# Hybrid two-layer decoder trunk on one core: query phase loaded by alternating chunks in a fixed order, norm squares moved to ScalarE

## The chip, the core and the metric

The kernel runs on one core of a Trainium2 chip. The metric is device microseconds of one execution. The core has TensorE (PE, with its weight loads as PEld), VectorE (DVE), ScalarE (ACT), GpSimd (POOL) and SyncE (SP), which issues most transfers; ScalarE's queue issues the rest.

## The reference, cut to what matters

The input x is 512 x 1024 float32. Two layers follow each other, and each adds a mixer and a SwiGLU feed-forward network to x, both behind an RMS norm.

```python
def rms_norm(x, g):
    y = x * rsqrt(mean(x * x, axis=-1, keepdims=True) + EPS)
    return y * g
for layer in range(2):
    h = rms_norm(x, norm_mix[layer])
    x = x + (even_mixer(h, ...) if layer == 0 else odd_mixer(h, ...))
    h = rms_norm(x, norm_ffn[layer])
    x = x + (silu(h @ w_gate) * (h @ w_up)) @ w_down
```

The even mixer projects h to queries, keys and values of a stick-breaking attention and to the three inputs of a short gated convolution; the odd mixer selects the 128 best keys of each query and attends to them. So there are four norms: one of the input x, and three of a sum that the kernel has just made. We number these three A (layer 0 mixer to feed-forward 0), B (feed-forward 0 to layer 1 mixer) and C (layer 1 mixer to feed-forward 1).

## The kernel before, in words

**Number format.** Every float32 operand is split into a high and a low part, and a product is three matmuls (`mm3`, L102 to L106): high by high, high by low, low by high. Weights arrive as `raw`; `new_weights` (L143) issues the load on SP, ScalarE casts the high part `wh` (L149), VectorE or GpSimd subtracts the low part `wl` (L150). Three buffers each hold `raw`, `wh` and `wl`. Activations lie feature by token in `xT`, in eight chunks of 128 features; `split` (L166) makes a chunk's high part on ScalarE, scaled by the norm's gain (L174), and its low part on VectorE (L175). The factor 1/rms of a token is put in behind the matmuls, so that they need not wait for it.

**The start.** `setup` (L305) builds constants, loads the first gains and issues `WARM` matmuls of a constant. `layer0_mix` (L533) then runs the query phase. `load_x` (L372) loads x in four loads of 256 features, transposes each chunk on TensorE by four transposes (L382), splits it and copies it to `xT` on ScalarE (L385). The query projection takes weights in four loads of two chunks; for each it runs four output blocks m of 128 features, two chunks each, into four PSUM banks: 96 matmuls in all. Then `first_rstd` (L389) sums the squares of x on VectorE (L396, four instructions), takes the reciprocal root on ScalarE (L401) with a Newton step on VectorE (L281 to L283), and builds the row form `rbc` by four diagonal tiles (L409) and matmuls by ones (L411). `stack` (L414) takes each query block out of its bank by two ScalarE copies (L420) and two VectorE subtractions (L424). The next projection's first block (the keys, `k_proj`) uses the bank of query block 0. `setup_rest` (L336) loads the other gains by six transfers on ScalarE's queue and transposes them (L345).

**What sets the order.** A scheduler places each engine's instructions from the program's order and its own estimate of when each is ready. Only where a `manual_schedule` region is open (layer 1's mixer, L749) does each named engine keep the order in which the program issues; instructions from outside the region may still fall between them. `slot()` (L229) is called after each `mm3` of the later projections and runs what `after(n, ...)` has put n slots ahead.

**Norms A, B and C.** `residual_proj` (L646) adds each of the eight output chunks to `xT` (L655, L657), splits it for the next layer, and calls `stats_add` (L264): GpSimd squares the chunk (L268, L272) and adds it to `ssq` (L273); for the last chunk ScalarE squares (L275) and VectorE adds (L276). `rstd_mm` (L285) is put `LAGR_FFN` = 6 slots behind the projection for A and C, `LAGR_MIX` = 7 for B: a matmul by ones (L289) sums `ssq` over the partitions, and root and Newton step give `rbc`. Eight slots later `rstd_cols` (L296) turns it into columns `rcol` by four small matmuls (L300). Feed-forward 0 uses `rbc` alone.

Of the kernel before, what the change touches and what calls it, by code (L numbers as in the profile page):

```python
# [8 lines left out]
F32 = mybir.dt.float32  # L9
F32R = mybir.dt.float32r  # L10
ALU = mybir.AluOpType
# [4 lines left out]
P = 128  # L16
# [3 lines left out]
TB = S // P  # L20
HID = 2816
HC = HID // P
WARM = 24
ORDER = None
RATE0, LAG0 = 0.8, 5
LAGR_FFN, LAGR_MIX = 5, 7
L1_ORDER = {mybir.EngineType.PE, mybir.EngineType.DVE, mybir.EngineType.Activation,
            mybir.EngineType.Pool}
LAG_W, LAG_KI, LAG_DOT, LAG_CH, LAG_TK, LAG_TQ, LAG_T1, LAG_N, LAG_C, LAG_LO, LAG_P, EXPS = 3, 8, 5, 4, 8, 6, 4, 8, 11, 2, 3, 1
LAG_Z = 14  # L30
LAG_K, T1P, B2, LAG_KLO, P1 = 2, 3, 'adbc', 2, 0
EARLY, SQ_ACT = 3, 0
# [7 lines left out]
FILL = -3e38  # L40
TAKEN = -3.4e38
ARENA_KB = 104.5

EARLY = 2
T1P = 4
# [6 lines left out]
B2 = 'dbca'  # L52
LAG_N = 8
LAG_TK = 8
LAGR_FFN = 6
LAG_KLO = 1
LAG_Z = 14
LAG_W = 4
# [17 lines left out]
class Net:  # L76
# [64 lines left out]
                 2, 512, lo) for k0 in range(0, kc, 2)]  # L141

    def new_weights(self, src, kk, n, lo):  # L143
        nc = self.nc
        raw = self.wraw.tile([P, kk, n], F32, name="raw", tag="raw")
        nc.sync.dma_start(raw, src)
        wh = self.wsp.tile([P, kk, n], F32R, name="wh", tag="wh")
        wl = self.wsp.tile([P, kk, n], F32R, name="wl", tag="wl")
        nc.scalar.copy(wh, raw)  # L149
        (lo or nc.vector).tensor_tensor(wl, raw, wh.bitcast(F32), op=ALU.subtract)  # L150
        return wh, wl
# [109 lines left out]
            self.slot()  # L261


    def stats_add(self, c):  # L264

        nc = self.nc
        if c == 0:
            nc.gpsimd.tensor_tensor(self.ssq, self.xT[:, c], self.xT[:, c], op=ALU.mult)  # L268
            return
        sq = self.cst.tile([P, S], F32, name="sqx", tag="sqx")  # L270
        if c < KC - 1:
            nc.gpsimd.tensor_tensor(sq, self.xT[:, c], self.xT[:, c], op=ALU.mult)  # L272
            nc.gpsimd.tensor_tensor(self.ssq, self.ssq, sq, op=ALU.add)  # L273
        else:
            nc.scalar.activation(sq, self.xT[:, c], AF.Square)  # L275
            nc.vector.tensor_tensor(self.ssq, self.ssq, sq, op=ALU.add)  # L276

    def newton(self, y, v, t, src=None):

# [5 lines left out]
    def rstd_mm(self):  # L285
# [50 lines left out]
    def setup_rest(self):  # L336
        nc, I = self.nc, self.I
        rows = self.rows2
        nc.scalar.dma_start(rows[0:16, :], I["norm_ffn"].rearrange("l (c p) -> (l c) p", p=P))
        nc.scalar.dma_start(rows[16:28, :], I["ev_conv_w"][0].rearrange("w (c p) -> (w c) p", p=P))  # L340
        for j in range(2):
            nc.scalar.dma_start(rows[28:29, j * 64:(j + 1) * 64], I["od_q_gain"])
            nc.scalar.dma_start(rows[29:30, j * 64:(j + 1) * 64], I["od_k_gain"])
        ps = self.bank("z", "pstat")
        nc.tensor.transpose(ps[:, 0:30], rows[0:30, :], self.ident[0:30, 0:30])  # L345
        nc.vector.tensor_copy(self.cols[:, 16:46], ps[:, 0:30])
        nc.vector.tensor_scalar(self.cols[:, 46:47], self.cols[:, 44:45], 0.125, None, op0=ALU.mult)
# [21 lines left out]
            nc.scalar.dma_start(self.F, ft)  # L369


    def load_x(self, xp):  # L372

        nc = self.nc
        xr = self.I["x"].rearrange("o (b p) d -> p (o b) d", p=P)
        xt = xp.tile([P, TB, D], F32, name="x_tm")
        for i in range(4):
            nc.sync.dma_start(xt[:, :, i * 256:(i + 1) * 256], xr[:, :, i * 256:(i + 1) * 256])
            for c in (2 * i, 2 * i + 1):
                ps = self.bank("z", "pstat")  # L380
                for tb in range(TB):
                    nc.tensor.transpose(ps[:, tb * P:(tb + 1) * P], xt[:, tb, c * P:(c + 1) * P],  # L382
                                        self.ident)
                self.split(self.xh3(c), ps, g=self.g_mix(0, c))
                nc.scalar.copy(self.xT[:, c], ps)  # L385
            self.x_tm = xt
            yield

    def first_rstd(self, xp):  # L389
# [15 lines left out]
        dg = xp.tile([P, S], F32, name="dg")  # L405
        ps = self.bank("z", "pstat")
        for tb in range(TB):
            t = slice(tb * P, (tb + 1) * P)
            nc.vector.tensor_scalar(dg[:, t], self.ident, self.rcol[:, tb:tb + 1], None,  # L409
                                    op0=ALU.mult)  # L410
# [122 lines left out]
    def layer0_mix(self):  # L533
# [7 lines left out]
        heads = []  # L541
        with self.tc.tile_pool(name="xin", bufs=1) as xp:

            loads = self.load_x(xp)
            ps = [self.acc() for _ in range(4)]
            next(loads)
            for k0 in range(0, KC, 2):
                next(loads, None)
                wh, wl = self.weights(W[k0 * P:(k0 + 2) * P, 0:512].rearrange(
                    "(k p) n -> p k n", p=P), 2, 512)  # L550
                for m in range(4):
                    c = slice(m * P, (m + 1) * P)
                    for k in range(2):
                        h, l = xs[k0 + k]
                        self.mm3(ps[m], wh[:, k, c], wl[:, k, c], h, l, k0 + k == 0,
                                 k0 + k == KC - 1)
            self.first_rstd(xp)
            for m in range(4):
                qs = self.R(32 + 4 * m, 2, S)
                self.stack([(qs[0][:, e], qs[1][:, e]) for e in range(2)], ps[m])  # L560
                heads.append(qs[0])
        self.setup_rest()
        self.bias_table()

# [4 lines left out]
        with self.tc.tile_pool(name="l0", bufs=1) as sp:  # L569
# [67 lines left out]
            for j in range(4):  # L637
# [3 lines left out]
            self.few_banks(None)  # L641
            att = [(self.R(32 + 4 * i, S)[0], self.R(34 + 4 * i, S)[0]) for i in range(4)]
            self.residual_proj(I["ev_w_out"][0], att + conv, self.xh3,
                               lambda c: self.g_ffn(0, c), pair=2)

    def residual_proj(self, W, ins, out3, gain, scale_r=False, tmp=None, pair=1, part=False,  # L646
                      lo=None):

        nc = self.nc

        def ev(m, ps):
            if scale_r:
                t = tmp.tile([P, S], F32, name="rt", tag="ft")
                nc.vector.tensor_tensor(t, ps, self.rbc, op=ALU.mult)
                nc.vector.tensor_tensor(self.xT[:, m], self.xT[:, m], t, op=ALU.add)  # L655
            else:
                nc.vector.tensor_tensor(self.xT[:, m], self.xT[:, m], ps, op=ALU.add)  # L657
            if not part:
                self.split(out3(m), self.xT[:, m], g=gain(m))
                self.stats_add(m)  # L660
        self.proj_fm(W, 0, D, ins, ev, pair=pair, lo=lo)
        if not part:
            self.after(LAGR_MIX if scale_r else LAGR_FFN, self.rstd_mm)


    def ffn(self, layer, xs, g0):
# [5 lines left out]
        with self.tc.tile_pool(name=f"ffn{layer}", bufs=2) as fp:  # L672
# [30 lines left out]
            if not last:  # L703
                self.plan(self.fm_tiles(Wd, 0, D, HC, 256, 4, 1, None) + self.l1_tiles())
                self.residual_proj(Wd, gs, self.xh3, lambda c: self.g_mix(1, c), scale_r=True,
                                   tmp=fp)
                return
            for half in range(2):
                def ev_d(tb, ps):
# [21 lines left out]
    def layer1_mix(self):  # L731
# [15 lines left out]
        with ExitStack() as es:  # L747
# [331 lines left out]
            self.residual_proj(Wo[512:1024], half[4:8], lambda c: out3[c],  # L1079
                               lambda c: self.g_ffn(1, c))  # L1080
        self.ffn(1, [(o[0], o[2]) for o in out3], 0)


# [47 lines left out]
```

## Time and profile before

| what | us |
|---|---|
| median of 3 runs | 1231.54 (1231.36 to 1231.57) |
| the profiled execution | 1230.06 |
| its span, first to last instruction | 1228.3 |
| TensorE busy in it | 1196.7 (97%) |
| VectorE, ScalarE, GpSimd busy | 669.5, 466.2, 189.3 |

Times in the rows are microseconds from the span's start. A timeline row gives start, duration, engine, line, operation, output from inputs, shape, count, and in brackets the idle time before it and what ended that. Matmul durations overlap: the distance from one start to the next is the pace. A float32 operand without the split is run in two passes and shows as two records.

### The profile page before, as it was taken

To read this page: it belongs to the slowest core of one execution; us is meant where nothing else is said; L and a number is where in the kernel's file an instruction comes from. 1 tells how busy PE (TensorE), PEld (TensorE's weight loads), DVE (VectorE), ACT (ScalarE), POOL (GpSimd) and SP (SyncE) were. 2 spreads that over 40 slices of the span, in tenths; PEclk is the share of its full clock that TensorE was granted. 3 is DMA by queue.
4 is the path that set the end of the run, shared out by engine and by line. 5 is a ranking of instruction groups with operands and counts; after the bars stand their busy time and mean duration, and the time that the engine had idled before them with its cause. 6 is when DMAs were issued, how large, how long until landed. Compare 5 with 4: busy or idle time off the path is not lost.

```text
span 1228.3 us, 14473 instructions
## 1 busy us (share of the span) xinstructions
PE 1196.7 (97%) x5573; PEld 982.4 (80%) x5573; DVE 669.5 (55%) x1064; ACT 466.2 (38%) x755; POOL 189.3 (15%) x228
## 2 busy tenths in 40 slices
PE   9999999999999999999999889998999999999998
PEld 8787878788888888888787678887888888888886
DVE  6769965634343343444589988757444444342322
ACT  5656733332233222222263379654322222322120
POOL 1334303200000000122135444226000000000000
PEclk9999999999999999999999999999999999999999
DMA  6231223333333332232223221112333233323330
GB/s 206 68 91 53 60 79 97 92 94 95 103 86 103 92 97 94 95 95 87 86 89 93 77 70 35 53 50 88 86 88 101 87 103 86 103 90 99 111 112 35
DMA packets 103637, 108.32 MB, mean 88 GB/s; under 512 B 4660, under 2 KB 89696, under 8 KB 103568
## 3 DMA queue, kind: packets, MB, share of 16 engines
q1 hardware_dynamic: 102768, 106.21, 29.0%
q10 hardware_dynamic: 800, 1.18, 0.3%
q8 instruction: 44, 0.72, 0.2%
q14 instruction: 25, 0.20, 0.1%
HBM read 105.24 MB, written 2.14 MB: 87 GB/s over the span
## 4 chain that ended last, share of the span: by engine, by line
PE 79%; DVE 12%; issue 5%; ACT 2%; POOL 2%; DMA 1%; ACTq 0%; POOLq 0%; DVEq 0%
PE acc L104 20%; PE acc L106 20%; PE acc L105 20%; PE acc L220 4%; PE acc L219 4%; PE acc L221 4%; DVE wl L150 2%; DVE w L825 1%; DVE L L828 1%; PE pt L1009 1%; DVE arena L175 1%; DVE om L458 1%; DVE xT L657 1%; PE z L433 1%; PE po L105 1%
## 5 line engine op out<-in xcount | busy, mean ns | idle before, releaser
L104 PE MATMUL acc<-arena,wh 128*128 128x512 f32 (+2 forms) x1176 | 468.1, 398 | 1.4 <-DVE xT L657 1.0
L106 PE MATMUL acc<-arena,wl 128*128 128x512 f32 (+2 forms) x1176 | 459.8, 391 | 0.0
L105 PE MATMUL acc<-arena,wh 128*128 128x512 f32 (+2 forms) x1176 | 456.7, 388 | 1.4 <-DVE arena L175 1.3
L150 DVE TENSOR_TENSOR wl<-raw,wh 128x1024 fp32r<-128x1024 f32 (+1 forms) x175 | 220.8, 1262 | 347.3 <-ACT wh L149 347.2
L149 ACT CAST wh<-raw 128x1024 fp32r<-128x1024 f32 (+1 forms) x191 | 198.6, 1041 | 462.7 <-issue 196.5
L106 PEld LDWEIGHTS acc<-arena,wl 128*128 128x128 f32 (+1 forms) x1176 | 220.7, 188 | 50.3 <-issue 0.2
L105 PEld LDWEIGHTS acc<-arena,wh 128*128 128x128 f32 (+1 forms) x1176 | 221.1, 188 | 47.4 <-DVE arena L175 2.3
L104 PEld LDWEIGHTS acc<-arena,wh 128*128 128x128 f32 (+1 forms) x1176 | 221.1, 188 | 45.1 <-DVE xT L657 2.1
L219 PE MATMUL acc<-wh,arena 128*128 128x512 f32 x272 | 108.9, 400 | 0.3 <-DVE arena L175 0.3
L220 PE MATMUL acc<-wl,arena 128*128 128x512 f32 x272 | 108.2, 398 | 0.0
L221 PE MATMUL acc<-wh,arena 128*128 128x512 f32 x272 | 108.1, 397 | 0.0
L221 PEld LDWEIGHTS acc<-wh,arena 128*128 128x128 f32 x272 | 51.4, 189 | 12.2
L219 PEld LDWEIGHTS acc<-wh,arena 128*128 128x128 f32 x272 | 51.5, 189 | 12.1 <-DVE arena L175 0.7
L220 PEld LDWEIGHTS acc<-wl,arena 128*128 128x128 f32 x272 | 51.5, 189 | 11.5
L683 DVE TENSOR_TENSOR ft<-acc,rbc 128x512 f32<-128x512 f32 x44 | 30.5, 692 | 55.2 <-PE acc L106 55.0
L268 POOL TENSOR_TENSOR ssq<-xT 128x512 f32<-128x512 f32 x3 | 3.5, 1169 | 327.8 <-DVE xT L655 274.0
L150 POOL TENSOR_TENSOR wl<-raw,wh 128x1024 fp32r<-128x1024 f32 x16 | 38.9, 2430 | 69.3 <-ACT wh L149 67.8
L685 ACT ACTIVATE fs<-ft 128x512 f32<-128x512 f32 x44 | 27.5, 629 | 52.2 <-DVE ft L683 52.2
L690 DVE TENSOR_TENSOR fp<-acc,fs 128x512 f32<-128x512 f32 x44 | 30.4, 692 | 28.5 <-PE acc L106 28.5
L433 PE MATMUL z<-arena 128*128 128x384 f32 (+3 forms) x120 | 41.2, 346 | 4.8 <-DVE mx L976 2.8
L976 DVE CUSTOM_DVE_ANT_0 L<-z,bias 128x128 f32<-128x128 f32 (+3 forms) x64 | 30.7, 486 | 18.2 <-PE z L975 17.6
L986 ACT ACTIVATE L<-L,mx 128x128 f32<-128x128 f32 (+3 forms) x64 | 35.8, 560 | 11.9 <-DVE sm L993 9.4
(205 smaller groups left out, 1285.9 us busy)
## 6 DMA issues: line engine op xcount, KB each, us to landing
raw<-in_ffn_w_gate_dram SPq DMA_DIRECT2D x44, 512.0 KB, 3.8
raw<-in_ffn_w_up_dram SPq DMA_DIRECT2D x44, 512.0 KB, 3.7
raw<-in_ffn_w_down_dram SPq DMA_DIRECT2D x42, 512.0 KB, 3.7
raw<-in_ev_w_in_dram SPq DMA_DIRECT2D x24, 512.0 KB, 3.9
raw<-in_od_w_in_dram SPq DMA_DIRECT2D x16, 512.0 KB, 3.5
raw<-in_ev_w_out_dram SPq DMA_DIRECT2D x8, 512.0 KB, 3.4
bias<-F SPq DMA_DIRECT2D x16, 256.0 KB, 3.2
raw<-in_od_w_out_dram SPq DMA_DIRECT2D x8, 512.0 KB, 3.4
```

The lines of the kernel that those rows point to most:

```text
L104: mm(ps, wh, xh, start=first, stop=False)
L105: mm(ps, wh, xl, start=False, stop=False)
L106: mm(ps, wl, xh, start=False, stop=last)
L149: nc.scalar.copy(wh, raw)
L150: (lo or nc.vector).tensor_tensor(wl, raw, wh.bitcast(F32), op=ALU.subtract)
L219: mm(ps[tb], h[:, t], wh[:, k], start=c == 0, stop=False)
L220: mm(ps[tb], h[:, t], wl[:, k], start=False, stop=False)
L221: mm(ps[tb], l[:, t], wh[:, k], start=False, stop=c == kc - 1)
L433: self.nc.tensor.matmul(z, qs, kd, start=True, stop=False)
L683: nc.vector.tensor_tensor(t, ps, self.rbc, op=ALU.mult)
L976: nc.vector.tensor_tensor_reduce(out=u["ls"][:, r], in0=z, in1=bias[h][:, 0:nk][:, ::-1], scale=1.0, scalar=FILL, op0=ALU.add, op1=ALU.max ...
L986: nc.scalar.activation(ls[:, r], ls[:, r], AF.Exp, bias=mx[:, r:r + 1], accum_out=sm[:, r:r + 1])
```

## The change

x and the query weights come in turn by spans of 1, 1, 2, 2 and 2 chunks: all five x loads and the first three weight loads are issued at the start. The phase from the first transpose to `first_rbc` stands in a `manual_schedule` region for TensorE, VectorE, ScalarE and GpSimd: a span's transposes, splits and `xT` copies are issued after block m = 1 of the span before it, its weight casts only after them, and `first_rstd`'s sums of squares after all five spans. The row form's matmuls are issued after the `stack` calls. `setup_rest` first writes its tile from `rcol`, so its six transfers wait for `first_rstd`. `WARM` goes from 24 to 15. ScalarE makes all norm squares; GpSimd keeps the additions of chunks 0 to 6; in A and C the last chunk's square and addition are issued ahead of its split, and squares alternate between two buffers. `rstd_mm` is put 8 slots behind in A, 9 in B, 11 in C. A has no `rstd_cols`. The layer 1 key index waits 10 slots (`LAG_KI`) in place of 8.

```diff
-WARM = 24
+WARM = 15
-LAGR_FFN, LAGR_MIX = 5, 7
+LAGR_FFN, LAGR_MIX = 5, 9
...
+X_SPANS = ((0, 1), (1, 2), (2, 4), (4, 6), (6, 8))
...
-LAGR_FFN = 6
+LAGR_FFN = 8
...
-    def stats_add(self, c):
+    def stats_add(self, c, free):
         if c == 0:
-            nc.gpsimd.tensor_tensor(self.ssq, self.xT[:, c], self.xT[:, c], op=ALU.mult)
+            nc.scalar.activation(self.ssq, self.xT[:, c], AF.Square)
             return
...
+        sq = (self.rbc if free and c % 2 else
+              self.cst.tile([P, S], F32, name="sqx", tag="sqx"))
+        nc.scalar.activation(sq, self.xT[:, c], AF.Square)
+        (nc.gpsimd if c < KC - 1 else nc.vector).tensor_tensor(self.ssq, self.ssq, sq, op=ALU.add)
...
-        self.after(8, self.rstd_cols)
+        if cols:
+            self.after(8, self.rstd_cols)
...
     def setup_rest(self):
+        nc.vector.tensor_copy(rows, self.rcol[0:32, 0:1].to_broadcast([32, P]))
...
+    def load_x(self, xp, W):
+        for i, (a, b) in enumerate(X_SPANS):
+            c = slice(a * P, b * P)
+            nc.sync.dma_start(self.x_tm[:, :, c], xr[:, :, c])
+            if i < 3:
+                raws.append(self.load_raw(W[c, 0:512].rearrange("(k p) n -> p k n", p=P),
+                                          b - a, 512))
+        return raws
+    def turn_x(self):
+        for a, b in X_SPANS:
+            for c in range(a, b):
+                ps = self.bank("z", "pstat")
+                for tb in range(TB):
+                    nc.tensor.transpose(ps[:, tb * P:(tb + 1) * P],
+                                        self.x_tm[:, tb, c * P:(c + 1) * P], self.ident)
                 self.split(self.xh3(c), ps, g=self.g_mix(0, c))
                 nc.scalar.copy(self.xT[:, c], ps)
             yield
+    def queries(self, W, raws):
+        turns = self.turn_x()
+        self.qps = ps = [self.acc() for _ in range(4)]
+        next(turns)
+        for i, (a, b) in enumerate(X_SPANS):
+            raw = raws[i] if i < 3 else self.load_raw(...)
+            wh, wl = self.halves(raw, b - a, 512)
+            for m in range(4):
+                c = slice(m * P, (m + 1) * P)
+                for k in range(a, b):
+                    h, l = xs[k]
+                    self.mm3(ps[m], wh[:, k - a, c], wl[:, k - a, c], h, l, k == 0, k == KC - 1)
+                if m == 1:
+                    next(turns, None)
...
+            raws = self.load_x(xp, W)
+            with self.tc.manual_schedule(engines=L1_ORDER):
+                self.queries(W, raws)
+                dg = self.first_rstd(xp)
                 for m in range(4):
...
+                    self.stack([(qs[0][:, e], qs[1][:, e]) for e in range(2)], self.qps[m])
+                self.first_rbc(dg)
...
             if not part:
+                first = m == KC - 1 and not scale_r
+                if first:
+                    self.stats_add(m, not scale_r)
                 self.split(out3(m), self.xT[:, m], g=gain(m))
-                self.stats_add(m)
+                if not first:
+                    self.stats_add(m, not scale_r)
...
-            self.after(LAGR_MIX if scale_r else LAGR_FFN, self.rstd_mm)
+            self.after(lagr, lambda: self.rstd_mm(cols))
```

`halves` is the second part of `new_weights` (the two L149 and L150 instructions), `load_raw` the first. Layer 0's output projection passes `cols=False`, the down projection of feed-forward 0 passes `lagr=LAGR_MIX`, layer 1's last output projection passes `lagr=11`.

## Rows read from the trace of the kernel before

**Rows 1.** The page: busy time, and shares of the chain that ended last.
```profile
PE 1196.7 (97%) x5573; PEld 982.4 (80%) x5573; DVE 669.5 (55%) x1064; ACT 466.2 (38%) x755; POOL 189.3 (15%) x228
...
PE 79%; DVE 12%; issue 5%; ACT 2%; POOL 2%; DMA 1%; ACTq 0%; POOLq 0%; DVEq 0%
```

**Rows 2.** TensorE's timeline of the query phase and the matmul behind it.
```profile
13.35 0.66 PE L382 MATMUL pstat<-eye,x_tm 128*128 128x128 f32 x4 [0.41 <-ACT xT L385]
...
24.59 1.03 PE L382 MATMUL pstat<-eye,x_tm 128*128 128x128 f32 x8
...
25.69 0.40 PE L105 MATMUL acc<-arena,wh 128*128 128x512 f32 x1
...
36.23 0.39 PE L106 MATMUL acc<-arena,wl 128*128 128x512 f32 x1
36.46 1.05 PE L411 MATMUL pstat<-dg,ones 128*128 128x128 f32 x8
...
37.61 0.50 PE L104 MATMUL acc<-arena,wh 128*128 128x512 f32 x1
```

**Rows 3.** Busy time by window (us, instructions), granted clock, DMA share, GB/s: the start.
```profile
0.00:7.00 7.00, 5.88 (x31) 5.88 (x32) 0.68 (x3) 1.28 (x1) 3.56 (x11) 1.00 0.61 177
```

**Rows 4.** ScalarE's timeline: splits, copies and weight casts.
```profile
14.04 0.69 ACT L174 ACTIVATE arena<-pstat,cols 128x512 fp32r<-128x512 f32 x1 [0.26 <-PE pstat L382]
...
24.59 1.05 ACT L149 CAST wh<-raw 128x1024 fp32r<-128x1024 f32 x1 [2.13 <-PE acc L105]
25.55 1.26 ACT L174 ACTIVATE arena<-pstat,cols 128x512 fp32r<-128x512 f32 x2
...
28.23 1.06 ACT L385 COPY xT<-pstat 128x512 f32<-128x512 f32 x2
...
582.05 0.62 ACT L149 CAST wh<-raw 128x512 fp32r<-128x512 f32 x1 [4.40 <-PE acc L105]
```

**Rows 5.** VectorE's timeline in and behind the query phase.
```profile
21.75 1.22 DVE L396 CUSTOM_DVE_ANT_0 junk<-x_tm 128x1024 f32<-128x1024 f32 x1
...
23.01 1.23 DVE L396 CUSTOM_DVE_ANT_0 junk<-x_tm 128x1024 f32<-128x1024 f32 x1
...
25.67 1.23 DVE L150 TENSOR_TENSOR wl<-raw,wh 128x1024 fp32r<-128x1024 f32 x1 [1.23 <-ACT wh L149]
...
28.36 0.16 DVE L281 TENSOR_TENSOR t<-rcol 128x4 f32<-128x4 f32 x1
...
29.10 0.87 DVE L409 TENSOR_SCALAR dg<-eye,rcol 128x128 f32<-128x128 f32 x4
...
33.74 4.22 DVE L424 TENSOR_TENSOR arena<-acc,arena 64x512 fp32r<-64x512 f32 x6 [0.45 <-ACT arena L420]
```

**Rows 6.** Transfers issued before 60 us: tile, queue, KB, us to landing.
```profile
ssq<-in_norm_ffn_dram ACTq DMA_DIRECT2D x1, 8.0 KB, 4.0
```

**Rows 7.** TensorE's timeline at norm A.
```profile
235.14 1.12 PE L289 MATMUL pstat<-ssq,ones 128*128 128x512 f32 x2 [0.38 <-DVE ssq L276]
...
242.07 0.40 PE L106 MATMUL acc<-arena,wl 128*128 128x512 f32 x1
...
243.37 0.51 PE L104 MATMUL acc<-arena,wh 128*128 128x512 f32 x1
```

**Rows 8.** TensorE's timeline at norm B.
```profile
599.99 0.39 PE L104 MATMUL acc<-arena,wh 128*72 128x512 f32 x1
...
605.59 0.52 PE L104 MATMUL acc<-arena,wh 128*128 128x384 f32 x1
```

**Rows 9.** Busy time by window, columns as in rows 3: norms B and C.
```profile
603.00:607.00 4.00, 4.00 (x10) 2.67 (x11) 1.72 (x3) 1.62 (x3) 0.00 (x0) 0.57 0.00 1
...
853.00:859.00 6.00, 2.28 (x9) 1.25 (x8) 4.84 (x5) 3.36 (x4) 2.42 (x2) 1.00 0.22 57
```

**Rows 10.** TensorE's timeline at norm C.
```profile
853.79 0.39 PE L106 MATMUL acc<-arena,wl 128*128 128x512 f32 x1
857.90 1.13 PE L289 MATMUL pstat<-ssq,ones 128*128 128x512 f32 x2 [3.72 <-DVE ssq L276]
```

More of the change, by code (lines that the diff above doesn't have):

```diff
@@ L143, in new_weights, with load_raw, halves @@
     def new_weights(self, src, kk, n, lo):
+        return self.halves(self.load_raw(src, kk, n), kk, n, lo)
+    def load_raw(self, src, kk, n):
+        raw = self.wraw.tile([P, kk, n], F32, name="raw", tag="raw")
+        self.nc.sync.dma_start(raw, src)
+        return raw
+    def halves(self, raw, kk, n, lo=None):
         nc = self.nc
-        raw = self.wraw.tile([P, kk, n], F32, name="raw", tag="raw")
-        nc.sync.dma_start(raw, src)
         wh = self.wsp.tile([P, kk, n], F32R, name="wh", tag="wh")
@@ L283, in newton, with rstd_mm @@
         nc.vector.scalar_tensor_tensor(y, t, 1.5, y, op0=ALU.add, op1=ALU.mult)
-    def rstd_mm(self):
+    def rstd_mm(self, cols=True):
         nc = self.nc
@@ L369, in bias_table @@
             nc.scalar.dma_start(self.F, ft)
-    def load_x(self, xp):
+    def load_x(self, xp, W):
         nc = self.nc
         xr = self.I["x"].rearrange("o (b p) d -> p (o b) d", p=P)
[L376 to L379, printed above, removed]
+        self.x_tm = xp.tile([P, TB, D], F32, name="x_tm")
+        raws = []
+        for i, (a, b) in enumerate(X_SPANS):
[6 more added lines that the diff above has]
+    def turn_x(self):
+        nc = self.nc
+        for a, b in X_SPANS:
+            for c in range(a, b):
                 ps = self.bank("z", "pstat")
                 for tb in range(TB):
-                    nc.tensor.transpose(ps[:, tb * P:(tb + 1) * P], xt[:, tb, c * P:(c + 1) * P],
-                                        self.ident)
+                    nc.tensor.transpose(ps[:, tb * P:(tb + 1) * P],
+                                        self.x_tm[:, tb, c * P:(c + 1) * P], self.ident)
                 self.split(self.xh3(c), ps, g=self.g_mix(0, c))
                 nc.scalar.copy(self.xT[:, c], ps)
-            self.x_tm = xt
             yield
+    def queries(self, W, raws):
+        xs = self.xs
+        turns = self.turn_x()
+        self.qps = ps = [self.acc() for _ in range(4)]
+        next(turns)
+        for i, (a, b) in enumerate(X_SPANS):
+            raw = raws[i] if i < 3 else self.load_raw(W[a * P:b * P, 0:512].rearrange(
+                "(k p) n -> p k n", p=P), b - a, 512)
+            wh, wl = self.halves(raw, b - a, 512)
[3 more added lines that the diff above has]
+                    h, l = xs[k]
+                    self.mm3(ps[m], wh[:, k - a, c], wl[:, k - a, c], h, l, k == 0,
+                             k == KC - 1)
+                if m == 1:
+                    next(turns, None)
     def first_rstd(self, xp):
@@ L405, in first_rstd, with first_rbc @@
         dg = xp.tile([P, S], F32, name="dg")
+        for tb in range(TB):
+            nc.vector.tensor_scalar(dg[:, tb * P:(tb + 1) * P], self.ident,
+                                    self.rcol[:, tb:tb + 1], None, op0=ALU.mult)
+        return dg
+    def first_rbc(self, dg):
+        nc = self.nc
         ps = self.bank("z", "pstat")
@@ L542, in layer0_mix @@
         with self.tc.tile_pool(name="xin", bufs=1) as xp:
[L544 to L550, printed above, removed]
-                for m in range(4):
[L552 to L561, printed above, removed]
+            raws = self.load_x(xp, W)
+            with self.tc.manual_schedule(engines=L1_ORDER):
+                self.queries(W, raws)
+                dg = self.first_rstd(xp)
+                for m in range(4):
+                    qs = self.R(32 + 4 * m, 2, S)
+                    self.stack([(qs[0][:, e], qs[1][:, e]) for e in range(2)], self.qps[m])
+                    heads.append(qs[0])
+                self.first_rbc(dg)
         self.setup_rest()
@@ L643, in layer0_mix @@
             self.residual_proj(I["ev_w_out"][0], att + conv, self.xh3,
-                               lambda c: self.g_ffn(0, c), pair=2)
+                               lambda c: self.g_ffn(0, c), pair=2, cols=False)
     def residual_proj(self, W, ins, out3, gain, scale_r=False, tmp=None, pair=1, part=False,
-                      lo=None):
+                      lo=None, lagr=LAGR_FFN, cols=True):
         nc = self.nc
@@ L705, in ffn @@
                 self.residual_proj(Wd, gs, self.xh3, lambda c: self.g_mix(1, c), scale_r=True,
-                                   tmp=fp)
+                                   tmp=fp, lagr=LAGR_MIX)
                 return
@@ L1079, in layer1_mix @@
             self.residual_proj(Wo[512:1024], half[4:8], lambda c: out3[c],
-                               lambda c: self.g_ffn(1, c))
+                               lambda c: self.g_ffn(1, c), lagr=11)
         self.ffn(1, [(o[0], o[2]) for o in out3], 0)
```

11 lines of the change are left out of this document (1 added, 10 removed).

## The prediction

> **What bounds the kernel now.** I read the page first: TensorE is busy for 1196.7 of 1228.3 us, and the chain that ended last runs on it for 79% [rows 1]. So time changes only where the change makes TensorE wait or spares it a wait or an instruction. Then I read TensorE's timeline where the change touches it: the start and norms A, B, C. The query phase, once running, leaves no gap: from 25.69 to 36.23 lie 46 steps of 0.229 us, and 37.61 sees the key projection begin right behind the row form [rows 2]. At the norms it waits: 0.38 us in A [rows 7], 3.72 in C [rows 10], and in B it needs 5.4 us for five matmuls and a sum [rows 8], partly because the clock fell [rows 9]. ScalarE's and VectorE's timelines give the prices [rows 4, 5].
>
> **The start, step by step.** The order in the region is fixed, so I follow each engine through it.
> - Warm-up: 31 TensorE records begin before 7.00 [rows 3], which is 15 warm matmuls at two records each and one more. The gains' transpose follows, so span 1's transposes start at about 7.2.
> - A span's chain: from its first transpose to the split's begin 0.69 (13.35 to 14.04) [rows 2, 4]. Then ScalarE makes, per chunk, a high part (1.26 / 2 = 0.63) and a copy (1.06 / 2 = 0.53), and only then casts the weights: 0.62 for one chunk, 1.05 for two [rows 4]. That is 2.5 us for a span of one chunk, 4.1 for two. VectorE's low part of the weights takes 1.23 more for two chunks [rows 5], about half for one (estimate), and the third matmul needs it.
> - Span 1: first matmul at 7.2 + 2.5 = 9.7, then 0.2 for the low part.
> - What covers a later span's chain is its own transposes, 0.44 per chunk (25.69 - 0.229 is when the first matmul behind the eight transposes began, 0.88 after 24.59 [rows 2]), and blocks m = 2 and 3 of the span before: 6 matmuls (1.37) or 12 (2.75).
> - Span 2: 2.5 - 0.44 - 1.37 = 0.7, and 0.2 for the low part: 0.9. Span 3: 4.1 - 0.88 - 1.37 = 1.8, and 1.23 less two matmuls (0.46) = 0.8: 2.6. Spans 4 and 5: 4.1 - 0.88 - 2.75 = 0.4, and 0.8: 1.2 each.
> - End of the queries: 9.7 + 96 x 0.229 (22.0) + 28 transposes at 0.11 (3.1) + 0.2 + 0.9 + 2.6 + 2.4 = 40.9. Before, it is 36.46.
> - The tail: the last weights' low part ends 22 matmuls before that, at 35.9. Only then may VectorE start the sums of squares: 4 x 1.26 (21.75 to 23.01), 0.5 for two short steps and the root (estimate from the 0.16 rows), 0.74 for Newton and scales (28.36 to 29.10), 0.87 for the diagonal tiles: 43.0. Then two subtractions of 4.22 / 6 = 0.70 free query block 0's bank [rows 5]: 44.4. The key projection needs that bank, so TensorE resumes at about 44.5 instead of 37.7. The row form's matmuls fall into this gap.
>
> **The start costs 6.8 us** (44.5 - 37.7), although the shorter warm-up lets it begin sooner: behind the first matmuls nothing is ready.
>
> Costed at nothing: the x and weight transfers, since span 5's data is wanted only near 31 us. The five smaller loads add SP issues, which no engine waits for. `setup_rest`'s six transfers now start when `rcol` stands (42.1); one such took 4.0 us to land [rows 6]. The gains' transpose would hold TensorE if the scheduler put it straight behind the row form: between 0 and 46.1 - 44.5 = 1.6 us. I take 0, because nothing near needs those gains and the scheduler places by its estimate of landing.
>
> **Norm A.** Without the four column matmuls (eight records) the matmuls run on: 243.37 - (242.07 + 0.229) = 1.07 us saved. With the sum two slots (1.4 us) later the 0.38 goes [rows 7]. **-1.5 us.** A miss would be a new wait of the feed-forward for `rbc`; its first gate block is finished 12 slots in and its bank is wanted only 32 slots in, and the root's chain needs some 8 slots.
>
> **Norm B.** From 599.99 + 0.23 to 605.59 are 5.4 us, with five matmuls (1.15) and the sum (1.0, its 1.12 less the overlap) of work [rows 7, 8]: 3.2 lost. From 603 to 607 the granted clock is 0.57 [rows 9], so the stretch from 605.59 loses a further 0.43 x 1.4 = 0.6. With GpSimd's square gone, VectorE reaches the low parts earlier; with the sum two slots later, its wait is covered. I leave 0.6 as the wait for one low part. **-3.2 us** (between -1.3, if only part of the waits goes and the clock still falls, and -3.8).
>
> **Norm C.** TensorE is free at 854.02 and starts the sum at 857.90: 3.9 us [rows 10]. Five slots more put 3.4 us of matmuls ahead of it, and the last addition no longer stands behind the split. **-3.9 us** (between -3.4 and -3.9). Seven more squares on ScalarE cost nothing: it is busy for 3.4 of the 6 us around this wait [rows 9]; should that cover go, a late high part costs one instruction, 0.6.
>
> **Sum:** +6.8 - 1.5 - 3.2 - 3.9 = -1.8. The profiled execution would go from 1230.06 to 1228.3. The median of the runs stands 1.48 above it, so I forecast **1229.7 us**. The measurement of this kernel can tell about 0.2% (2.5 us) from no change.
>
> **Rivals.**
> - *The start costs nothing*: the region does not bind ScalarE and VectorE as its text says, or weight casts and sums of squares slip ahead. Then spans follow each other as they do from 25.69 to 36.23 [rows 2]: 9.7 + 22.0 + 3.1 = 34.8, the sums of squares lie beside the matmuls, and the tail ends near 37.7 as now. Only the norms remain: -8.6, **1222.9 us**. For it: ScalarE has room. Against: the order is written out.
> - *The clock falls in the start* (the slower side). The row: behind two short waits in B the granted clock was 0.57 for 4 us, so mostly the lower of its levels (1.2 and 2.4 GHz), a loss of 1.7; behind C's 3.72 us it stayed 1.00 [rows 9, 10]. The start gets three such places: 2 us ahead of the first matmul, 2.6 in span 3, 3.4 at the tail. Three falls cost 5.2: +3.4, **1234.9 us**; two leave it within 0.2%, so the third decides. The Trainium skill ("TensorE: Matmul & The Clock Gate", "HAM oscillation — how this bites in real kernels") says that waits between groups of matmuls put the engine back to its slow clock, so that each next group starts cold; by that rule every one of the three places would pay, and this rival would be the forecast. The trace agrees in B and not in C.
> - *The late gains hold TensorE* for the 1.6 us above: -0.2, **1231.3 us**.
> - *The norms' waits move on instead of going*, to the column matmuls of B or C, which need `rbc` eight slots behind the sum. At full pace B's eight slots are only about 5.3 us. Half of B's and C's gain lost is +3.6: +1.8, **1233.3 us**.
>
> **How the numbers follow.** Chances: the forecast 0.52 (its own range 1226.5 to 1232.8: the start between +4.5 and +9, the norms' bounds), the start for nothing 0.23, the clock 0.10, the late gains 0.08, the norms moved on 0.07. Faster by over 0.2% are the start for nothing and a third of the forecast's range, in all 0.42; slower by over 0.2% is the clock and a little of the forecast, 0.12; the rest, 0.46, lies within. The range goes from 1221.8, below the start for nothing, to 1233.3.
>
> **What would show it.** In the changed profile: TensorE's first projection matmul near 9.7; gaps ahead of span 3 ended by the weight casts (L149's successor) and their low parts; the last query matmul near 41; the key projection released by VectorE's subtraction near 44.5; no column matmuls in A; the sums by ones without a wait in A and C; granted clock near 1.00 at B. The forecast is wrong if queries end before 38 us, or if the sum in C still waits over 1 us.

## The result, and the profile after

The kernel after takes 1248.15 us (median of 4 runs, 1246.57 to 1248.82), the kernel before 1231.45 beside it (1230.56 to 1231.57): a ratio of 1.0135 (95% interval 1.0118 to 1.0153), 16.7 us slower where 1.8 us faster was forecast. The profiled execution, the shortest of the four at 1246.57 us, has a span of 1244.9 us against 1228.3 [rows 1].

The page of the kernel after, busy time and the granted clock by fortieths of the span:

```profile
PE 1201.4 (97%) x5547; PEld 983.7 (79%) x5547; DVE 651.1 (52%) x1065; ACT 477.5 (38%) x777; POOL 156.8 (13%) x207
...
PEclk8899999999999999999999999999999999999999
```

TensorE has 26 instructions less than before and is busy 4.7 us more, and its clock is short in the first two fortieths (62 us). There the time went. TensorE's timeline of that stretch, kernel after (answers to [rows 2]):

```profile
10.74 0.50 PE L105 MATMUL acc<-arena,wh 128*128 128x512 f32 x1 [3.67 <-ACT wh L156]
...
17.09 0.50 PE L105 MATMUL acc<-arena,wh 128*128 128x512 f32 x1 [1.09 <-ACT wh L156]
...
24.59 0.50 PE L105 MATMUL acc<-arena,wh 128*128 128x512 f32 x1 [3.29 <-ACT wh L156]
...
35.14 0.75 PE L105 MATMUL acc<-arena,wh 128*128 128x512 f32 x1 [1.93 <-ACT wh L156]
...
45.56 0.50 PE L105 MATMUL acc<-arena,wh 128*128 128x512 f32 x1 [1.92 <-ACT wh L156]
...
51.74 0.39 PE L107 MATMUL acc<-arena,wl 128*128 128x512 f32 x1
56.39 2.05 PE L452 MATMUL pstat<-dg,ones 128*128 128x128 f32 x8 [4.26 <-DVE dg L443]
58.40 0.77 PE L105 MATMUL acc<-arena,wh 128*128 128x512 f32 x1
```

Each of the five spans begins with a wait for its weights' cast, the last query matmul starts at 51.74 instead of 36.23, and the keys at 58.40 instead of 37.61: 20.8 us later. The windows of the same stretch (columns as in [rows 3]) show why it is more still:

```profile
11.40:14.60 3.20, 3.20 (x10) 2.57 (x10) 0.01 (x1) 0.17 (x1) 0.00 (x0) 0.50 0.73 217
24.60:28.20 3.60, 3.26 (x8) 2.16 (x9) 1.19 (x1) 0.00 (x0) 0.00 (x0) 0.55 0.27 75
35.00:38.30 3.30, 3.08 (x7) 1.98 (x8) 1.23 (x1) 0.09 (x1) 0.00 (x0) 0.53 0.22 31
56.00:62.50 6.50, 6.11 (x18) 5.04 (x19) 6.32 (x13) 3.73 (x7) 0.00 (x0) 0.50 0.33 90
```

Four times the granted clock is at or near the lower level (1.2 of 2.4 GHz). By the clock's share in each, the windows lose 1.6 + 1.6 + 1.6 + 3.3 = 8.1 us; that is the most that the falls can have cost, since a slow stretch that shortens a later wait costs less (`e4_fill` measures it). Of the last window 2.0 us lie behind 58.40, so the start costs 22.8 us in all. By the last transposes of the stick-breaking attention (159.3 us into the span before, 182.1 after) the lag is that 22.8. The norms then take most of what they promised: 21.0 behind A, 18.5 behind B (compared matmul by matmul; it holds from 622 us into the span before, when both kernels run the same order again). Layer 1's mixer loses 1.1 (19.6), C brings the lag to 15.6, and the last down-projection adds 1.1: 16.7. TensorE's timeline at the norms, kernel after (answers to [rows 7, 8, 10]):

```profile
258.81 1.02 PE L293 MATMUL pstat<-ssq,ones 128*128 128x512 f32 x2
...
622.00 0.45 PE L106 MATMUL acc<-arena,wh 128*72 128x512 f32 x1 [0.63 <-DVE arena L182]
...
623.74 1.02 PE L293 MATMUL pstat<-ssq,ones 128*128 128x512 f32 x2
...
877.03 1.02 PE L293 MATMUL pstat<-ssq,ones 128*128 128x512 f32 x2
```

None of the three sums waits any more, and of B's waits 0.63 for one low part is left.

**Why a span takes so long** is read from ScalarE's timeline, kernel after (answers to [rows 4]):

```profile
6.79 1.28 ACT L181 ACT_TABLE_LOAD   x1 [6.79 <-DVE cols L339]
8.08 0.69 ACT L181 ACTIVATE arena<-pstat,cols 128x512 fp32r<-128x512 f32 x1
...
19.51 0.69 ACT L181 ACTIVATE arena<-pstat,cols 128x512 fp32r<-128x512 f32 x1 [2.47 <-PE pstat L400]
21.02 0.58 ACT L403 COPY xT<-pstat 128x512 f32<-128x512 f32 x1 [0.82 <-DVE arena L182]
21.50 0.69 ACT L181 ACTIVATE arena<-pstat,cols 128x512 fp32r<-128x512 f32 x1
23.01 0.58 ACT L403 COPY xT<-pstat 128x512 f32<-128x512 f32 x1 [0.82 <-DVE arena L182]
23.49 1.05 ACT L156 CAST wh<-raw 128x1024 fp32r<-128x1024 f32 x1
30.05 0.69 ACT L181 ACTIVATE arena<-pstat,cols 128x512 fp32r<-128x512 f32 x1 [5.52 <-PE pstat L400]
```

A chunk's copy waits 0.82 us for VectorE's low part, which reads the same PSUM tile; so a chunk takes 2.0 us (19.51 to 21.50), not 1.16. Behind the span ScalarE stands idle for 5.52 us until the next transposes, although it could have cast the next weights (`e7_ahead` does). VectorE's timeline behind the last span, kernel after (answers to [rows 5]):

```profile
46.68 1.22 DVE L432 CUSTOM_DVE_ANT_0 junk<-x_tm 128x1024 f32<-128x1024 f32 x1
...
47.82 1.22 DVE L157 TENSOR_TENSOR wl<-raw,wh 128x1024 fp32r<-128x1024 f32 x1
...
50.10 1.22 DVE L157 TENSOR_TENSOR wl<-raw,wh 128x1024 fp32r<-128x1024 f32 x1
...
53.65 1.22 DVE L157 TENSOR_TENSOR wl<-raw,wh 128x1024 fp32r<-128x1024 f32 x1
...
55.96 0.86 DVE L443 TENSOR_SCALAR dg<-eye,rcol 128x128 f32<-128x128 f32 x4
```

Between and behind the four sums of squares stand three low parts (1.14 us from start to start) of the next projection's weights, which nobody needs yet, and TensorE waits 4.26 us for the diagonal tiles.

So the theory: the start's cost has three sources, the copies that wait in a fixed order, the clock that falls behind the waits, and the low parts in the tail.

### The profile page after: what moved, and what is told of

Same layout as the page of the kernel before. It is cut to its first block, busy times and chain, and to the rows that moved or that the text cites. A ratio compares the mean times of both kernels' runs of the same rounds, so it can differ in the third digit from the quotient of the medians.

```text
span 1244.9 us, 14423 instructions
## 1 busy us (share of the span) xinstructions
PE 1201.4 (97%) x5547; PEld 983.7 (79%) x5547; DVE 651.1 (52%) x1065; ACT 477.5 (38%) x777; POOL 156.8 (13%) x207
## 4 chain that ended last, share of the span: by engine, by line
PE 80%; DVE 11%; issue 4%; ACT 2%; POOL 2%; DMA 1%; POOLq 0%; DVEq 0%; ACTq 0%
PE acc L105 21%; PE acc L107 20%; PE acc L106 20%; PE acc L226 4%; PE acc L228 4%; PE acc L227 4%; DVE w L861 1%; DVE L L864 1%; DVE wl L157 1%; PE pt L1045 1%; DVE om L499 1%; PE z L474 1%; DVE arena L182 1%; PE po L106 1%; DVE ssq L864 1%
## 5 line engine op out<-in xcount | busy, mean ns | idle before, releaser
L105 PE MATMUL acc<-arena,wh 128*128 128x512 f32 (+2 forms) x1176 | 469.9, 400 | 13.0 <-ACT wh L156 11.9
L157 DVE TENSOR_TENSOR wl<-raw,wh 128x1024 fp32r<-128x1024 f32 (+1 forms) x176 | 212.9, 1210 | 363.2 <-ACT wh L156 363.2
L105 PEld LDWEIGHTS acc<-arena,wh 128*128 128x128 f32 (+1 forms) x1176 | 222.3, 189 | 58.2 <-ACT wh L156 13.9
L280 POOL TENSOR_TENSOR ssq<-ssq,sqx 128x512 f32<-128x512 f32 x12 | 18.6, 1547 | 375.1 <-ACT sqx L279 375.1
L178 ACT CAST arena<-fp 128x512 fp32r<-128x512 f32 x36 | 22.2, 617 | 46.8 <-DVE fp L726 46.8
```

Source lines behind the costliest of these rows:

```text
L105: mm(ps, wh, xh, start=first, stop=False)
```

## The experiments

Edits are against the kernel after. "Against the kernel after" means the difference of the two ratios to the kernel before, times 1231.5 us.

**e1_norms_only and e2_start_only: the two halves of the change.** The first has the start of the kernel before and all else of the change, the second has the start of the change, with the norms, slots and column roots of the kernel before.

```diff
-WARM = 15
+WARM = 24
...
-            raws = self.load_x(xp, W)
-            with self.tc.manual_schedule(engines=L1_ORDER):
-                self.queries(W, raws)
+            loads = self.load_x(xp)
...
```

> The changed norms A, B and C with the start of the kernel before (its loads, 24 warm matmuls, no fixed order, gains loaded at once). Theory (the whole loss is the start; the norms gain what was forecast): 1231.5 - 1.8 - 3.1 - 4.0 = 1222.6, up to 1225.3 if the 1.7 us that the changed kernel lost inside layer 1 and the 1.0 at the end belong to the norms. Rival (the norms' waits only move on): 1229 to 1233.

Measured: 1224.39 us, ratio 0.9929 (0.9909 to 0.9949), that is -8.7 us. No sum by ones waits.

The second half's edit, in short:

```diff
-LAGR_FFN, LAGR_MIX = 5, 9
+LAGR_FFN, LAGR_MIX = 5, 7
...
-LAGR_FFN = 8
+LAGR_FFN = 6
...
-        nc.scalar.activation(sq, self.xT[:, c], AF.Square)
...
+            nc.gpsimd.tensor_tensor(sq, self.xT[:, c], self.xT[:, c], op=ALU.mult)
...
-        if cols:
-            self.after(8, self.rstd_cols)
+        self.after(8, self.rstd_cols)
```

> The changed start with the norms of the kernel before. Theory: the start alone costs 20.8 us to the first key matmul and 2 more until the clock is back, so 1231.5 + 22.8 = 1254.3. Rival (start and norms hinder each other, for example by the scheduler's other placing): 1246 to 1250.

Measured: 1255.70 us, ratio 1.0182 (1.0163 to 1.0201), that is +22.4 us. The halves add to +13.7, and 16.7 was measured for both: the 3.0 between them is within the intervals, which are some 2.4 us to each side of each half. The whole loss is in the start.

**e3_copy_first: ScalarE's copy ahead of VectorE's low part.** The low part then waits for the copy, and VectorE has the time.

```diff
-                self.split(self.xh3(c), ps, g=self.g_mix(0, c))
+                (hr, hf, lr), g = self.xh3(c), self.g_mix(0, c)
+                nc.scalar.activation(hr, ps, AF.Copy, scale=g)
                 nc.scalar.copy(self.xT[:, c], ps)
+                nc.vector.scalar_tensor_tensor(lr, ps, g, hf, op0=ALU.mult, op1=ALU.subtract)
```

> The changed kernel with one swap: ScalarE's copy of a chunk of x out of its bank is issued ahead of VectorE's low part from the same bank, not behind it. Theory (the copy waits 0.82 us for the low part in each of eight chunks, and the weight cast behind it holds TensorE): TensorE's five waits for the cast shrink by 0.8, 0.8, 1.6, 1.6 and 1.6, which is 6.4 us, and some of the clock's falls go too: 1237 to 1242 instead of 1248.2. Rival (the copy is not on the path): 1247 to 1249.

Measured: 1237.21 us, ratio 1.0040 (1.0026 to 1.0054): 11.7 us less than the kernel after. ScalarE's timeline of span 3 in this kernel:

```profile
17.42 0.69 ACT L403 ACTIVATE arena<-pstat,cols 128x512 fp32r<-128x512 f32 x1 [2.60 <-PE pstat L400]
18.01 0.58 ACT L404 COPY xT<-pstat 128x512 f32<-128x512 f32 x1
18.47 0.70 ACT L403 ACTIVATE arena<-pstat,cols 128x512 fp32r<-128x512 f32 x1
...
19.52 1.07 ACT L156 CAST wh<-raw 128x1024 fp32r<-128x1024 f32 x1
```

Its waits on TensorE (total, times, longest):

```profile
PE pstat L454 <- DVE dg L445: 4.3, 1, 4.3
PE acc L105 <- ACT wh L156: 4.2, 2, 2.7
```

And the granted clock of most of the query phase, a window of the same kernel:

```profile
15.00:40.00 25.00, 21.81 (x100) 16.04 (x100) 11.92 (x15) 11.42 (x17) 0.00 (x0) 1.00 0.29 83
```

A chunk now takes 1.05 us, the waits for casts fall from 11.9 us in five places to 4.2 in two, and two of the four falls of the clock are gone (15 to 40 us stays at 1.00). The gain is larger than the 8 x 0.82 = 6.6 us of the copies' waits; the two falls that went with them (3.2 us by their windows) are likely most of the rest. The tail's 4.3 us stays.

**e4_fill: TensorE kept busy through the waits.** In front of each span's matmuls, and of the row form, it multiplies constants into a PSUM bank that holds nothing then (16, 4, 14, 8, 8 and 18 matmuls). The result of them is not used.

```diff
             wh, wl = self.halves(raw, b - a, 512)
+            self.fill_pe((16, 4, 14, 8, 8)[i])
...
                 dg = self.first_rstd(xp)
+                self.fill_pe(18)
```

> The changed kernel with matmuls of a constant put into TensorE's waits (16, 4, 14, 8 and 8 ahead of the five spans, 18 ahead of the row form), a little shorter than each wait at full clock, into a bank that nothing else uses then. Theory (the clock falls behind these waits and the falls cost 1.6, 1.6, 1.6 and 3.2 us): granted clock 1.00 from 7 to 60 us and 8 us less, 1240. Rival (the slow stretches are not on the path, the waits for the casts absorb them): clock 1.00 but 1246 to 1248.

Measured: 1241.07 us, ratio 1.0064 (1.0039 to 1.0090): 8.7 us less than the kernel after, with 68 matmuls more (136 records on TensorE, two for each). Two of the four windows that ran at half clock, in this kernel:

```profile
35.00:38.30 3.30, 3.28 (x19) 2.81 (x19) 0.00 (x0) 0.24 (x1) 0.00 (x0) 1.00 0.53 159
56.00:62.50 6.50, 6.50 (x28) 5.33 (x29) 5.52 (x9) 1.40 (x3) 0.00 (x0) 1.00 0.06 12
```

The clock is at its upper level in all windows from 6 to 63 us, so the falls come from TensorE's idleness. What they cost is less than the 8.1 us of the windows. In the two profiled executions the lag at the attention's last transposes is 18.5 against 22.8: 4.3 us, or 5.4 if one counts from the first transpose of x, which came 1.1 later in this execution (7.48 against 6.42). By spans, 1.3 + 1.2 + 1.0 came back from the three falls in the queries, not 1.6 each. The rest was time for which TensorE would otherwise have waited: its waits for low parts grew from 0.9 to 1.6 us, and behind the row form it now waits 0.95 us for query block 0's bank. So the rival was right in part. A further 2.0 us of the profiled difference lie in layer 1's mixer and the last down-projection, where this edit changes nothing.

**e5_sums_early: two sums of squares in span 3 and two in span 4**, ahead of the last weights' low parts.

```diff
             wh, wl = self.halves(raw, b - a, 512)
+            for tb in {2: (0, 1), 3: (2, 3)}.get(i, ()):
+                self.square_sum(tb)
```

> The changed kernel with the four sums of squares of x issued on VectorE inside the spans (two in span 3, two in span 4) and no longer behind all five. Theory (behind the last query matmul TensorE waits for the four sums and the weight splits between them, and the clock falls there): TensorE resumes at about 53 us instead of 58.4 and the slow stretch behind it goes, so 7 us less, 1241. Rival (the tail is bound by emptying the first query bank, not by the sums): TensorE still waits 3 us or more there, 1246 or above.

Measured: 1241.65 us, ratio 1.0073 (1.0052 to 1.0094): 7.6 us less than the kernel after. The five waits for casts stay (11.3 us). TensorE's timeline at the row form in this kernel:

```profile
55.47 1.05 PE L457 MATMUL pstat<-dg,ones 128*128 128x128 f32 x8
```

The row form follows the last query matmuls without a wait and at full pace, so the tail's 4.26 us and the longest of the falls are gone together. The clock is not cured, though: in this execution it falls behind the wait for the cast of span 5 as well (1.94 us; granted clock 0.57 from 47.9 to 51.9), where it stayed up in the kernel after.

**e6_free_order: the same loads and the same program, without the fixed order.**

```diff
-            with self.tc.manual_schedule(engines=L1_ORDER):
+            with ExitStack():
```

> The changed kernel without the fixed order of the query phase: same chunks, same alternating loads, 15 warm matmuls, changed norms, the scheduler places. Theory (the loss is the written order, not the chunks or the loads): the weight casts go ahead of the chunks' copies again and the sums of squares lie beside matmuls, 1222 to 1228. Rival (small chunks or the alternating loads are at fault): 1240 or above.

Measured: 1226.06 us, ratio 0.9948 (0.9933 to 0.9963). The scheduler casts weights as they land, and the keys start at 41.16. Two waits are left on TensorE's timeline of the start (and one fall of the clock, 0.59 from 12 to 20 us); the third row is from VectorE's:

```profile
9.17 0.23 PE L338 MATMUL pstat<-eye,ssq 16*128 16x16 f32 x1 [2.64 <-DVE eye L322]
...
12.36 2.08 PE L105 MATMUL acc<-arena,wh 128*128 128x512 f32 x4 [1.94 <-ACT arena L181]
...
8.90 0.22 DVE L322 CAST eye<-ssq 128x128 fp32r<-128x128 f32 x1
```

So it is the order that costs, not the smaller loads: 23.0 us less with the same loads. The first wait is for the identity tile `eye`: here the scheduler put its cast on VectorE behind the low parts of the first two weight spans, which wait for loads, at 8.90; in the kernel after it stands at 1.73. The kernel is still 2.3 us above e1_norms_only, with intervals that overlap.

**e7_ahead: a fixed order that runs ahead.** The copy goes before the low part, the next span's cast before its transposes, both behind block m = 0, and the sums of squares into spans 3 and 4.

```diff
+        ahead = cast(0)
         next(turns)
         for i, (a, b) in enumerate(X_SPANS):
-            wh, wl = self.halves(raw, b - a, 512)
+            wh, wl = ahead
...
-                if m == 1:
+                if m == 0:
+                    if i < len(X_SPANS) - 1:
+                        ahead = cast(i + 1)
                     next(turns, None)
+                    for tb in {2: (0, 1), 3: (2, 3)}.get(i, ()):
+                        self.square_sum(tb)
```

> The changed kernel with a fixed order that runs ahead: copy before low part, the weight cast of the next span issued before that span's transposes, both behind block 0 instead of block 1 of the span before, and the sums of squares inside spans 3 and 4. Theory: first matmul near 8 us, no wait above 1 us in the phase, last query matmul near 34, keys from about 35.5 (2 us earlier than the kernel before): 1224.4 (norms alone) less 2 is 1222. Rival (a fixed order costs in itself, for example because weights of the next projection fall between): 1228 or above.

Measured: 1221.09 us, ratio 0.9909 (0.9894 to 0.9924), the lowest median of all. TensorE's timeline of the query phase in this kernel:

```profile
8.29 0.49 PE L105 MATMUL acc<-arena,wh 128*128 128x512 f32 x1 [0.78 <-ACT arena L405]
...
9.55 0.51 PE L106 MATMUL acc<-arena,wh 128*128 128x512 f32 x1 [0.77 <-DVE arena L407]
...
34.55 1.05 PE L467 MATMUL pstat<-dg,ones 128*128 128x128 f32 x8
35.36 0.47 PE L105 MATMUL acc<-arena,wh 128*128 128x512 f32 x1
```

The two waits shown are the only ones, the granted clock is 1.00 from 5 to 60 us, and the keys start 2.2 us earlier than before [rows 2]. So loads in turn do pay when each engine's order lets it work ahead. Against e1_norms_only the gain is 2.5 us by the ratios, with intervals that overlap.

**e8_old_lags and e9_old_squares: what the norms' gain is made of.** Both have the start of before and no column roots in A. The first keeps the new squares with the old slots (6, 7, 6, and 8 for the key index), the second the old squares with the new slots (8, 9, 11). Against e1_norms_only the edits are, first:

```diff
-LAGR_FFN, LAGR_MIX = 5, 9
+LAGR_FFN, LAGR_MIX = 5, 7
...
-LAGR_FFN = 8
+LAGR_FFN = 6
...
-                               lambda c: self.g_ffn(1, c), lagr=11)
+                               lambda c: self.g_ffn(1, c))
```

and second:

```diff
-        nc.scalar.activation(sq, self.xT[:, c], AF.Square)
...
+        if c < KC - 1:
+            nc.gpsimd.tensor_tensor(sq, self.xT[:, c], self.xT[:, c], op=ALU.mult)
...
-                first = m == KC - 1 and not scale_r
...
                 self.split(out3(m), self.xT[:, m], g=gain(m))
+                self.stats_add(m)
```

> The changed norms with the start of the kernel before, but the sum by ones back at 6, 7 and 6 slots and the key index at 8. What is left of the norms' change: squares on ScalarE, last square ahead of the split, no column roots in A. Theory (two parts each carry some of C: the squares bring the last addition about 3 us nearer, the slots cover the rest): a wait of about 1 us returns in C and up to 0.6 in B, 1225.5 to 1227 against 1224.4. Rival (the slots alone do it): C waits over 3 us again, 1228 or above.

> The start of the kernel before, the later slots of the kernel after (8, 9 and 11), no column roots in A, but the squares as before: GpSimd squares chunks 0 to 6, and the last chunk's square and addition stand behind its split. Theory: the squares on ScalarE and the last square ahead of the split carry most of what the norms give, since with them alone, at the old slots, the time was 1223.8. Then the later slots alone cover the sum in A and C, but GpSimd still shares VectorE's time ahead of B, so that B keeps a wait of about 1.5 for a low part, and C keeps at most 0.5 of its 3.7: 1224.5 to 1226.5. Rival, either cure alone is enough (whichever part is there, the sum is ready before TensorE asks for it): within 1 us of 1223.8, and no wait of over 0.7 for the sum anywhere.

Measured: 1223.78 us, ratio 0.9931 (0.9911 to 0.9950), and 1223.96 us, ratio 0.9941 (0.9927 to 0.9956). Neither can be told from e1_norms_only (0.9929). TensorE's timeline of e8_old_lags at B and C:

```profile
600.42 1.12 PE L293 MATMUL pstat<-ssq,ones 128*128 128x512 f32 x2 [0.59 <-DVE ssq L280]
...
852.13 1.12 PE L293 MATMUL pstat<-ssq,ones 128*128 128x512 f32 x2
```

And of e9_old_squares:

```profile
600.86 0.45 PE L106 MATMUL acc<-arena,wh 128*72 128x512 f32 x1 [1.32 <-DVE arena L182]
...
855.40 1.12 PE L296 MATMUL pstat<-ssq,ones 128*128 128x512 f32 x2 [0.30 <-DVE ssq L283]
```

Both times came out below the ranges expected (1225.5 to 1227, and 1224.5 to 1226.5). C's 3.72 us [rows 10] goes to nothing with the squares alone, where about 1 was expected, and to 0.30 with the slots alone, as expected. Either cure is enough at C. In e9_old_squares B keeps a wait of 1.32 us for a low part, as expected, but the time does not show it: the waits that differ are within what these runs can tell (2.4 us).

**e10_warm24: 24 warm matmuls in the kernel after.**

```diff
-WARM = 15
+WARM = 24
```

> The kernel after with 24 warm matmuls in place of 15, nothing else. Theory: the shorter warm-up hides nothing, since ScalarE's table load and casts set the first matmul: with 9 more warm matmuls (2.8 us in the profile, warm end 9.15 against 6.3) span 1's transposes start 2.8 later at most, of which some lies beside the table load; the falls of the clock come from the waits behind it and stay. 1248.2 to 1251. Rival, the warm-up being too short makes the first fall (11.4 to 14.6): then that stretch is at full pace, 1.6 us come back, and the time is 1247 to 1249.5, with the granted clock at 1.00 in the 3 us behind the first projection matmul.

Measured: 1249.61 us, ratio 1.0147 (1.0130 to 1.0164), 1.5 us more than the kernel after, intervals overlapping. The first matmul comes at 13.63, 2.9 later, behind the same wait of 3.67 us, and the falls stay. Two windows of this kernel:

```profile
14.00:18.00 4.00, 4.00 (x15) 3.11 (x15) 0.47 (x2) 0.69 (x1) 0.00 (x0) 0.68 0.48 131
...
24.00:32.00 8.00, 4.70 (x10) 3.33 (x11) 1.98 (x2) 2.39 (x4) 0.00 (x0) 0.68 0.23 67
```

The shorter warm-up is not what lets the clock fall.

## Why the prediction was wrong in the start and right in the norms

**Norms: right.** Forecast -1.5, -3.2 and -3.9 us; measured by the lag -1.8, -2.5 and -4.0, and -8.7 by e1_norms_only where the three terms make -8.6. The rival that the waits move on is not seen at any `rbc`. B's term, 0.7 too large but inside its bounds, took the fall of the clock there for a part of B. It is not a fixed part: in e2_start_only's profile, with the norms of before, B has the same two waits as before (1.32 and 0.58 us) and the granted clock stays at 1.00 (628 to 632 us), while behind C's 3.71 us it falls (0.78 from 882 to 886). So the 1.00 at B in the kernel after, the sign that I had asked for, proves little. The terms were also too sure in whom they credit: slots and squares each suffice (e8, e9).

**The start: the step that failed is the span's chain.** It took "a copy 0.53" for each chunk from a row of two copies without a wait, and let the low part go beside it. So it made 4.1 us for a span of two chunks, where spans 3, 4 and 5 took 5.72 each (from the transposes at 18.87, 29.42 and 39.84 to the first matmuls at 24.59, 35.14 and 45.56): 1.6 more, two waits of 0.82. The trace of before already held the answer, in rows that I had passed over. ScalarE's timeline, kernel before:

```profile
17.08 0.59 ACT L385 COPY xT<-pstat 128x512 f32<-128x512 f32 x1 [0.34 <-DVE arena L175]
...
21.21 1.25 ACT L385 COPY xT<-pstat 128x512 f32<-128x512 f32 x2 [0.79 <-DVE arena L175]
```

There the copies could slip behind the next chunk's high part, so two chunks shared one wait; in the fixed order each chunk pays 0.82. The two reads of one PSUM tile are never side by side in these traces, in either order (e3 turns the wait to VectorE). The Trainium skill ("PSUM — Partial Sum Buffer", "PSUM bank collisions raise a hardware error") says that the compiler makes two engines wait for each other when they touch the same partitions of one bank, two reads included. The rows agree; no run here tried them together.

The terms, forecast and measured:

| step | forecast | measured |
|---|---|---|
| first matmul | 9.7 | 10.74 |
| waits for casts in spans 2 to 5 | 0.7 + 1.8 + 0.4 + 0.4 = 3.3 | 1.09 + 3.29 + 1.93 + 1.92 = 8.2 |
| queries end | 40.9 | 51.97 (51.74 + 0.23) |
| last query weights' low part ends, to the keys | 44.5 - 35.9 = 8.6 | 58.40 - 46.68 = 11.7 |
| keys | 44.5 | 58.40 |
| half clock behind that | 0 | 2.0 |

- First matmul: 1.0 late. The transposes began 0.8 sooner than forecast (6.42 against 7.2), but from there the chain took 4.3 us in place of 2.5: the table load of 1.28 us ahead of ScalarE's first split, which was not in the chain, made that split 1.0 later, and the copy waited its 0.82.
- Queries: 10.0 us more between the first matmul and the end (41.2 against 31.2). The casts' waits make 4.9 of it and three falls of the clock 4.8 by their windows; the low parts' waits were forecast too large (2.8 against 0.9). The 2.2 left are mostly the waits' edges: a bracket counts from a matmul's modelled end, 0.16 behind its pace (0.39 less 0.229), and the first step behind a wait takes 0.34 instead of 0.229, which over six waits is 1.6.
- Tail: 2.8 us more from the queries' end to the keys (6.4 against 3.6). The order fixes what the region holds, and the next projection's weights are outside it; their low parts stepped in between the sums of squares. I had named "instructions from outside the region may still fall between them" of the order and not priced it.

Together 13.9, and 2.0 of half clock make 15.9, against 22.8 - 6.8 = 16.0. The direction of each step (first matmul behind its cast, gaps ahead of span 3, keys late) was right; the sizes were not.

**The clock rival** was right in kind and had a tenth of the chance. It counted three falls for 5.2 us; there were four, for 8.1 us by the windows and 5.4 by e4_fill, since the waits were longer and one more. Waits of 3.67, 3.29, 1.93 and 4.26 us are followed by a fall. The wait of 1.92 at 45.56 is not, nor was C's 3.72 [rows 10]. e4_fill shows that TensorE's idleness is the cause, and the length of a single wait does not tell which falls. Nor does its place: the same wait ahead of span 5 (1.92 to 1.94 us) is followed by a fall in the profiles of e2, e5 and e10 (granted clock 0.57, 0.57 and 0.59 in the 4 us from it), and the same wait at C in that of e2. The start of e2 is that of the kernel after, and its C that of the kernel before, so one execution can have a fall that another of the same code has not. The Trainium skill ("TensorE: Matmul & The Clock Gate", "HAM oscillation — how this bites in real kernels") tells of a loop in which the matmuls behind every wait start cold. In the start of the kernel after that held in four of six waits over 1 us.

**The other rivals.** That the start costs nothing is refuted: the region binds. e6_free_order comes nearest to it, with the region gone. That the late gains hold TensorE is refuted: their transpose is at 69.54 us and waits for nothing.

**Two losses outside the start.** Layer 1's mixer loses its 1.1 us where the granted clock falls (0.50 from 752 to 754 us, 0.64 from 754 to 756); the kernel before ran the same matmuls at 1.00 (734 to 736). The norms are not behind it: e1, e4, e7 and e9, which have all or part of the changed norms, do not have it. The last 1.1 us is a wait of TensorE for VectorE (1.00 us, at 1182.13), and VectorE itself waits there for the store of an earlier output tile. VectorE's timeline, kernel after and kernel before:

```profile
1181.32 1.41 DVE L747 SCALAR_TENSOR_TENSOR fo<-acc,rcol,xT 128x512 f32<-128x512 f32 x2 [4.88 <-DMA out_dram<-fo]
...
1164.60 1.41 DVE L711 SCALAR_TENSOR_TENSOR fo<-acc,rcol,xT 128x512 f32<-128x512 f32 x2 [3.71 <-DMA out_dram<-fo]
```

TensorE's wait is there in e3, e5, e6 and e7 as well (0.9 to 1.9 us), and not in e1, e2, e4, e8, e9 and e10, so no edit tried here goes with it. Why the store takes longer in some executions stays open.

## What to carry to other kernels

Before writing an order by hand, walk the chain of one stage with the waits of the rows, not only with their durations: a scheduler's order hides waits (two engines on one PSUM tile) that a fixed order pays each time, and it is not closed to instructions from outside it. In a fixed order, let each engine issue what is ready for the next stage (the weight cast) ahead of what must wait for this one. Where a stage makes TensorE wait several times within some tens of microseconds, put a price on the clock: here the falls cost some 5 us (8.1 by the windows at the low level) beside 16.2 us of waits (11.9 for casts, 4.3 in the tail).

## What the runs showed of the hardware that I had not expected

Two waits of the same length (1.93 and 1.92 us, ten microseconds apart, each behind twelve matmuls at full pace) had different ends: the clock fell behind the first and stayed behind the second, and in e2_start_only, whose start is the same code, it fell behind the second too. And matmuls whose results nobody uses paid: with 68 of them the kernel was 8.7 us faster, 5.4 of it seen in the start's trace.
